# Half of the next stage's norm moved beside an earlier output projection, side work pinned on four engines, statistics a pair later

## The chip, the cores and the metric

The kernel runs on one core of a Trainium2 chip. The metric is the time of one execution on the device in microseconds (us). Five engines of the core matter: PE (TensorE: matmuls, and its weight loads, PEld), DVE (VectorE), ACT (ScalarE), POOL (GpSimd) and SP (SyncE, which here only issues DMAs). Each engine works through its own instructions in a fixed order; engines and DMAs wait for each other through semaphores.

## The reference

One layer of a decoder trunk, then a final norm, on x of 2048 tokens by 1024 channels in float32. Cut to what matters:

```python
h = rmsnorm(x, norm1)
q, k, v, b_gate, c_gate, hc, p = split(h @ w_in)      # 512 128 128 256 256 256 256
attn = sliding_window_attention(q, k, v, sinks, rel_bias)   # window 128, 8 heads
conv = b_gate * causal_depthwise_conv3(c_gate * hc)
pool = per-group map of (trailing mean over 2/4/8/16 - p)
x = x + concat(attn, conv, pool) @ w_out
h2 = rmsnorm(x, norm2)
x = x + square(relu(h2 @ w1)) @ w2                    # 1024 -> 4096 -> 1024
return rmsnorm(x, final_norm)
```

## The kernel before

Everything is held transposed: channels lie on the 128 partitions, tokens along the free axis. Each fp32 product is made of three matmuls on high and low parts (`mm3`: hi·hi, hi·lo, lo·hi), so that one 128x512 tile over 1024 input channels is 24 matmuls of 128x512. High parts are casts on ACT (`wh`, `xh`), low parts are subtractions on POOL for the weights (`wl`, L253) and on DVE for the activations (`xl`, L406).

**Token blocks.** The first stages work on four blocks of 512 tokens, b = 0 to 3. The projection of a block (`proj`, L504; PSUM tiles `pj`) has 14 tiles of 24 matmuls, in the order IN_ORDER; the first ones are k and v, and the loop variable n counts the rest from 0. Beside them run eight attention units, one per n from 0 on: scores on PE (`sc`), scale plus bias on DVE (`s`, L581), maximum on DVE (L588), exponentials on ACT, the reciprocal of the sum and a scaling on DVE (`rd` L593, `s` L594), transposes on PE (`pt`), their high and low parts on ACT and DVE (`pth`, `ptl`, L608), the product with v on PE (`av`), and the heads' output (`ao`, L624). Conv and pool mixers (`do_pmix`: `ppm` on PE, `mxl` on DVE) run on the side. The q tiles' low parts `ql` go through a DMA before the scores can use them.

**Output projection of a block** (`out_proj`, L715; PSUM tiles `po`): eight tiles c = 0 to 7 of 24 matmuls on the mixed heads `mxh`, `mxl`. After each, DVE adds the residual (`xo`, L724), a DMA stores the result to the buffer `x1s` in DRAM, and ACT and POOL sum the squares for the second norm (`acc`, L732). Beside the same eight tiles runs the first norm of block b+1: squares and their sum (c = 0, 1), then `norm_rstd` at c = 2 (a matmul with ones, `pst_n`, and twelve small DVE operations `nt`, `nv`, `ny`, `r` at L316 to L325 that make the inverse root), a transpose on PE (`pr_n`, L333) and a store of the row to DRAM (`row_n`) at c = 3, its load broadcast to 128 partitions (`rb`) at c = 4, and the scaled activations `hf` (L404) with their parts `xh`, `xl` (L405, L406) from c = 5 on, which the projection of block b+1 multiplies.

**The next stage's norm.** The MLP's first stage works in two passes of 1024 tokens with seven products of half-size blocks (names T1 to T4, B11, B21, B22; PSUM tiles `bT`, `bB`), the sums and differences of which are prepared beforehand in DRAM (`x2s_T`, `x2s_B`). For the first pass (blocks 0 and 1) this is `first_blocks(k, step)` for k = 0 to 3. Step 0 loads four 128x512 tiles `xb` from `x1s`; step 1 scales them by the norm's row (four DVE operations, L809, with the broadcast rows `rb2`, loaded once by `first_rows`) and stores three of them; step 2 subtracts four times (`sub`, L763) and stores four results. Over all k that is 16 tile loads, two row loads, 16 scalings, 16 subtractions and 28 stores. In block 3, `first_load` and `first_take` read these back beside its output projection. The tiles `xb` take the place of the norm's input tiles `xr`, which the last block no longer needs.

**What sets the order.** The code is written in one order and a list scheduler with engine estimates places each instruction on its engine; what is in a `tc.issue_after(instruction)` block goes behind that instruction on that instruction's engine, and other engines are not bound by it. DMAs in `late` are put out at the next `w_next` (weights, taken `LEAD` ahead) or `flush`. The table FIRST gives for each k the values of n (in block 3) for its three steps:

```python
FIRST = ((0, 1, 2), (0, 3, 4), (3, 5, 6), (5, 7, 8))
...
            if b + 1 == NB:
                with tc.issue_after(latest[0].ins):
```

`latest[0]` is the last matmul of a projection tile, an instruction of PE.

**After the blocks.** PE runs the MLP's first stage, where events are keyed by (pass, group, step): `on(key, f)`. `norm2_rstd` for the last block (`pst_n`), `norm2_row` and `norm2_bcast` (the second pass's row) are such events. The low part `hlB`, `hlT` of what the first products use is made at L967. The second stage (`o`) ends with the final norm: the residual add, squares on ACT and their sum on POOL (`acc`, L942), the sum over partitions (`pst_n`), a broadcast (`pbc_n`), eight scalings on DVE (L1152) and eight stores on SP (L1156). The last part of this is done for the last 256 tokens alone.

Of the kernel before, what the change touches and what calls it, by code (L numbers as in the profile page):

```python
# [2 lines left out]

# [1 line left out]

# [60 lines left out]
ON_DVE = ((2, 5), (5,))  # L66
SUM_POOL = ("S1", "S2")

FIRST = ((0, 1, 2), (0, 3, 4), (3, 5, 6), (5, 7, 8))

NEARLY = 5

# [7 lines left out]
def f32(ap):  # L80
    return ap.bitcast(F32)
# [3 lines left out]
def tile_trunk(  # L85
# [12 lines left out]
):  # L98
    nc = tc.nc
    pe, act, dve, gp, sp = nc.tensor, nc.scalar, nc.vector, nc.gpsimd, nc.sync  # L100

    cst = ctx.enter_context(tc.tile_pool(name="cst", bufs=1, side="left"))
    wp = ctx.enter_context(tc.tile_pool(name="wp", bufs=2, side="left"))
# [164 lines left out]
    def flush():  # L268

        while late:  # L270
            late.pop(0)()

    def mm3(ps, hi, lo, xh, xl, first, last):
        pe.matmul(ps, hi, xh, start=first, stop=False)  # L274
        pe.matmul(ps, hi, xl, start=False, stop=False)  # L275
        return pe.matmul(ps, lo, xh, start=False, stop=last)  # L276


    prm = cst.tile([P, NPAR], F32, name="prm")
# [26 lines left out]

        return [min(o, w - P) for o in range(0, w, P)]

    def rstd_of(acc, r, offs, psp, tag, name):

        n = r.shape[-1]
        ps = psp.tile([P, T], F32, tag=tag, name=f"pst_{name}")
        for j, o in enumerate(offs):
            pe.matmul(ps[:, j : j + 1], acc[:, o : o + P], ones, start=True, stop=True)
        v, y, t = [cst.tile([P, 6], F32, tag=f"n{a}", name=f"n{a}_{name}", bufs=2)[:, :n] for a in "vyt"]
        dve.tensor_scalar(out=t, in0=ps[:, :n], scalar1=EPS, scalar2=None, op0=ALU.add)  # L316
        dve.tensor_scalar(out=v, in0=ps[:, :n], scalar1=EPS, scalar2=-0.5, op0=ALU.add, op1=ALU.mult)
        dve.tensor_scalar(
            out=y.bitcast(I32), in0=t.bitcast(I32), scalar1=-0.5, scalar2=1597463007.0,
            op0=ALU.mult, op1=ALU.add,  # L320
        )
        for it in range(3):
            dve.tensor_tensor(out=t, in0=y, in1=y, op=ALU.mult)
            dve.tensor_tensor(out=t, in0=t, in1=v, op=ALU.mult)
            dve.scalar_tensor_tensor(  # L325
                out=(r if it == 2 else y), in0=t, scalar=1.5, in1=y, op0=ALU.add, op1=ALU.mult
            )
# [152 lines left out]
    gp.memset(pp[:, :, 0:16], 0.0)  # L480

    first = {}

    latest = [None]

    def start_first(tiles):

        ws = [(w_next(0), w_next(0)) for _ in tiles]
# [10 lines left out]
    def proj(b, i, mid=None, bank=None):  # L499
        if b == 0 and i in first:  # L500
            ps = first[i]
            flush()
        else:
            xh, xl = xhl[b]  # L504
            ps = ps_mm.tile([P, T], F32, tag="mm", name=f"pj{b}_{i}") if bank is None else bank
            for k in range(KC):
                if k % HC == 0:
                    hi, lo = w_next()
                if k == HC and mid:
                    mid()  # L510
                latest[0] = mm3(ps, hi[:, k % HC], lo[:, k % HC], xh[:, k], xl[:, k], k == 0, k == KC - 1)
        return ps

    def scaled(b, i, ps):
# [271 lines left out]

        return plain, sums

    def first_rows():

        rb2[0] = [pB.tile([P, T], F32, tag=t, name=f"rb2_0_{t}") for t in ("rb", "acc")]
        for n in range(2):
            row_load(rb2[0][n], "n2", n * TH)

# [2 lines left out]
    def first_blocks(k, step):  # L797

        if step == 0:
            first_blk[k] = [pA.tile([P, T], F32, tag="xr", name=f"xb{k}_{n}", bufs=KC) for n in range(4)]  # L800
            for n, t in enumerate(first_blk[k]):
                a = n % 2 * TH
                sp.dma_start(t, x1s[k + n // 2 * HC][:, a : a + TH])
            return
        plain, sums = norm2_put(0, k, first_blk[k])
        if step == 1:
            for n, t in enumerate(first_blk[k]):
                m = PG2 + k + n // 2 * HC
                dve.scalar_tensor_tensor(  # L809
                    out=t, in0=t, scalar=prm[:, m : m + 1], in1=rb2[0][n % 2], op0=ALU.mult, op1=ALU.mult  # L810
                )
# [29 lines left out]
    for b in range(NB):  # L841
# [16 lines left out]
        for n, i in enumerate(IN_ORDER[NPRE:]):  # L858
            if n < KC and b + 1 < NB:
                norm_load(b + 1, n)  # L860

            def mid(n=n):
                if 2 <= n < 10:
                    st2[n] = att_trans(*st1.pop(n - 2))

            ps = proj(b, i, mid)
            if b and n == 1:
                norm2_row(b - 1, ps_tr, "tr", tmp(f"row2_{b}"))
            if 2 <= n < 10:
                av = att_av(*st2.pop(n))  # L870
            evac[i](b, scaled(b, i, ps))
            if 2 <= n < 10:
                att_out(*av, dve if n > 5 else gp)
            if n < 8:
                st1[n] = att_scores(b, *units[n])
            if n == 5:
                do_pool(b, 0)
            elif n == 7:
                do_pool(b, 1)
                do_pmix(b, 0)  # L880
            elif n == 9:
# [257 lines left out]
    def final_rstd(p, n, cs):  # L1139
        w = cs.stop - cs.start  # L1140
        offs = starts(w)
        r = cst.tile([P, 6], F32, tag="nr3", name=f"r3_{p}_{n}_{cs.start}", bufs=2)[:, : len(offs)]
        rstd_of(acc3[p, n][:, cs], r, offs, psb, "b", f"n3_{p}_{n}_{cs.start}")
        r3[p, n, cs.start] = r

    def final_bcast(p, n, cs):
        w = cs.stop - cs.start
        rb3[p, n, cs.start] = bcast(r3[p, n, cs.start], w, psb, "b", f"n3_{p}_{n}_{cs.start}")

    def final_mul(p, n, f, cs):  # L1150
# [5 lines left out]
        late.append(lambda: sp.dma_start(outT[f * P : (f + 1) * P, a + cs.start : a + cs.stop], t))  # L1156

    ev = {}
    full = slice(0, TH)
# [155 lines left out]
```

## Time and profile before

| | us |
|---|---|
| three runs of the kernel | 1935.1, 1942.73, 1940.79 (median 1940.79) |
| the profiled execution | 1936.93 |
| its span on the core | 1935.2 |
| busy: PE, DVE, POOL, ACT | 1892.6, 1123.6, 1020.0, 895.9 |
| granted PE clock, mean | 0.99 |

The span is what the trace covers; 1.73 us of the profiled execution lie outside it. In a row of a timeline the columns are: start and duration in us, engine, line, operation, out<-in, partitions x elements and type, count, and in brackets the idle time just before on that engine with what ended it. A row over a stretch of time (of the windows view) has start:end, length, then the busy time and number of instructions of PE, PEld, DVE, ACT and POOL, the granted PE clock, the share of the DMA engines and GB/s. A group's row has its count, and then busy us and mean ns of one.

### The profile page before, as it was taken

The page shows a single profiled execution, that of the slowest core. Times are in us where ns is not written, and L with a number is a line of the kernel's source. Part 1 is how long each engine was busy: PE and PEld are TensorE (multiplying, and loading weights), DVE is VectorE, ACT ScalarE, POOL GpSimd, SP SyncE. Part 2 cuts the span into 40 slices and gives each one's busy share as a digit, 9 for nine tenths or more (in the row PEclk, how much of TensorE's full clock was granted, in tenths as well). Part 3 has the DMA queues.
Part 4 walks back from the last instruction along what each step waited for, and adds up shares of the span by engine and source line. Part 5 has one row for each costly group of instructions (what it writes and reads, how often), then busy time and mean ns, then how long its engine had stood idle before and what let it go on. Part 6 is the DMA issues. An engine that isn't in the chain of part 4 may idle for free.

```text
span 1935.2 us, 25620 instructions
## 1 busy us (share of the span) xinstructions
PE 1892.6 (98%) x8507; PEld 1527.8 (79%) x8507; DVE 1123.6 (58%) x1423; ACT 895.9 (46%) x1640; POOL 1020.0 (53%) x748
## 2 busy tenths in 40 slices
PE   8999999999899999999999999999999999999997
PEld 5877887887687788888888888888888888888887
DVE  5785686585888577756574444442425264533465
ACT  5664674564367344554575545442323222225332
POOL 5666557565463655654464444434565665526521
PEclk9999999999899999999999999999999999999998
DMA  7327316425935779756685655578777566645344
GB/s 255 102 65 225 108 61 217 126 66 174 300 117 178 233 272 335 255 197 212 216 288 194 196 185 189 186 270 279 235 231 240 191 218 200 221 123 169 96 158 134
DMA packets 194136, 373.34 MB, mean 193 GB/s; under 512 B 22167, under 2 KB 30420, under 8 KB 194004
## 3 DMA queue, kind: packets, MB, share of 16 engines
q1 hardware_dynamic: 193768, 371.62, 59.6%
q8 instruction: 67, 1.10, 0.2%
q14 instruction: 65, 0.53, 0.1%
q10 hardware_dynamic: 236, 0.09, 0.0%
HBM read 248.41 MB, written 116.93 MB: 189 GB/s over the span
## 4 chain that ended last, share of the span: by engine, by line
PE 83%; DVE 7%; DMA 6%; issue 2%; ACT 1%; POOL 1%; SPq 1%; DVEq 0%; POOLq 0%; ACTq 0%
PE o L274 11%; PE o L275 11%; PE o L276 11%; PE bT L275 6%; PE bT L276 6%; PE bT L274 6%; PE bB L275 5%; PE bB L274 5%; PE bB L276 5%; PE pj L275 4%; PE pj L276 4%; PE pj L274 4%; DMA x1s<-xo 1%; PE pt L604 1%; DVE xl L406 1%
## 5 line engine op out<-in xcount | busy, mean ns | idle before, releaser
L253 POOL TENSOR_TENSOR wl<-wr,wh 128x512 fp32r<-128x512 f32 x354 | 499.2, 1417 | 502.4 <-ACT wh L252 462.1
L252 ACT CAST wh<-wr 128x512 fp32r<-128x512 f32 x416 | 254.3, 617 | 362.5 <-PE bT L275 66.9
L763 DVE TENSOR_TENSOR bl<-br,bh 128x1024 fp32r<-128x1024 f32 (+2 forms) x144 | 186.8, 1300 | 324.7 <-ACT bh L1111 323.8
L275 PE MATMUL o<-bl,wh 128*128 128x512 f32 (+1 forms) x960 | 363.4, 381 | 0.0
L276 PE MATMUL o<-bh,wl 128*128 128x512 f32 (+1 forms) x960 | 362.7, 381 | 0.0
L274 PE MATMUL o<-bh,wh 128*128 128x512 f32 (+1 forms) x960 | 351.1, 381 | 0.0
L275 PEld LDWEIGHTS o<-bl,wh 128*128 128x128 f32 x960 | 180.9, 188 | 38.3 <-DVE bl L763 0.2
L276 PEld LDWEIGHTS o<-bh,wl 128*128 128x128 f32 x960 | 180.8, 188 | 38.2
L274 PEld LDWEIGHTS o<-bh,wh 128*128 128x128 f32 x960 | 176.3, 188 | 38.0
L276 PE MATMUL bT<-hhT,wl 128*128 128x512 f32 x512 | 203.7, 398 | 0.0
L275 PE MATMUL bT<-hlT,wh 128*128 128x512 f32 x512 | 203.6, 398 | 0.0
L274 PE MATMUL bT<-hhT,wh 128*128 128x512 f32 x512 | 203.4, 398 | 0.0
L274 PE MATMUL pj<-xh,wh 128*128 128x512 f32 x440 | 176.7, 403 | 10.6 <-ACT wh L252 6.7
L275 PE MATMUL pj<-xl,wh 128*128 128x512 f32 x440 | 177.5, 403 | 6.1 <-DVE xl L406 5.8
L276 PE MATMUL pj<-xh,wl 128*128 128x512 f32 x440 | 176.2, 401 | 0.0
L253 POOL TENSOR_TENSOR wl<-s,wh 128x512 fp32r<-128x512 f32 x64 | 91.2, 1426 | 141.5 <-ACT wh L252 130.9
L252 ACT CAST wh<-s 128x512 fp32r<-128x512 f32 x64 | 39.7, 621 | 250.1 <-PE o L275 249.9
L275 PE MATMUL bB<-hlB,wh 128*128 128x512 f32 x384 | 152.3, 397 | 0.7 <-DVE hlB L967 0.7
L274 PE MATMUL bB<-hhB,wh 128*128 128x512 f32 x384 | 152.5, 397 | 0.0
L1111 ACT CAST bh<-br 128x1024 fp32r<-128x1024 f32 (+2 forms) x144 | 123.2, 857 | 63.3 <-PE o L276 57.6
L276 PE MATMUL bB<-hhB,wl 128*128 128x512 f32 x384 | 152.0, 396 | 0.0
L220 POOL TENSOR_TENSOR s<-wr,wr 128x512 f32<-128x512 f32 x64 | 128.5, 2008 | 14.9 <-DMA wr<-in_w_dram 10.2
(188 smaller groups left out, 3388.0 us busy)
## 6 DMA issues: line engine op xcount, KB each, us to landing
wr<-in_w_dram SPq DMA_DIRECT2D x256, 256.0 KB, 3.8
hop_T<-s SPq DMA_DIRECT2D x128, 256.0 KB, 3.1
wr<-in_win_dram SPq DMA_DIRECT2D x112, 256.0 KB, 4.4
hop_B<-h SPq DMA_DIRECT2D x96, 256.0 KB, 3.3
br<-hop_B SPq DMA_DIRECT2D x48, 512.0 KB, 4.4
br<-hop_T SPq DMA_DIRECT2D x48, 512.0 KB, 4.3
wr<-in_wout_dram SPq DMA_DIRECT2D x64, 256.0 KB, 2.9
wr<-ss_T SPq DMA_DIRECT2D x48, 256.0 KB, 2.8
```

Of the source, the lines that this page charges most:

```text
L220: gp.tensor_tensor(out=t, in0=a, in1=b, op=op)
L252: act.copy(hi, src)
L253: eng.tensor_tensor(out=lo, in0=src, in1=f32(hi), op=ALU.subtract)
L274: pe.matmul(ps, hi, xh, start=first, stop=False)
L275: pe.matmul(ps, hi, xl, start=False, stop=False)
L276: return pe.matmul(ps, lo, xh, start=False, stop=last)
L406: dve.tensor_tensor(out=xl[:, k], in0=hf, in1=f32(xh[:, k]), op=ALU.subtract)
L604: pe.transpose(ps[:, m * P : (m + 1) * P], s[:, m, kh * P : (kh + 1) * P], ident)
L763: return dve.tensor_tensor(out=out, in0=a, in1=b, op=ALU.subtract)
L1111: mark["act"] = act.copy(hi, src)
```

## The change

The norm for k = 0 and 1 (`first_rows` and two of the four `first_blocks`) is moved out of block 3's projection and into the output projection of block 2 (b + 2 == NB), where the tiles `pth`, `ptl`, `q0` and `q1` of the attention are not in use. For k = 2 and 3 it stays in block 3, at other values of n, with a second pair of row loads. The order of this work is now tied by `behind()` to the latest instruction on each of ACT, DVE, POOL and SP, and no longer to one of PE. The second norm's statistics at the start of the MLP come one group later. At the kernel's end the last 256 tokens' four squares are no longer added up on POOL: PE sums them in PSUM, with five matmuls for each of two columns in place of one, and the final stores alternate between the queues of SP and ACT.

```diff
-FIRST = ((0, 1, 2), (0, 3, 4), (3, 5, 6), (5, 7, 8))
+FIRST = ((), (), (0, 2, 3), (2, 4, 5))
+BEFORE = ((0, 1, 2), (1, 2, 3))
...
+    sides = {e.engine for e in (act, dve, gp, sp)}
...
+    @contextmanager
+    def behind():
+        with ExitStack() as order:
+            seen = set()
+            for ins in reversed(nc.cur_bb.bb.instructions):
+                if ins.engine in sides and ins.engine not in seen:
+                    seen.add(ins.engine)
+                    order.enter_context(tc.issue_after(ins))
+                    if len(seen) == len(sides):
+                        break
+            yield
...
-    def rstd_of(acc, r, offs, psp, tag, name):
+    def rstd_of(accs, r, offs, psp, tag, name):
...
+        accs = accs if isinstance(accs, list) else [accs]
         for j, o in enumerate(offs):
-            pe.matmul(ps[:, j : j + 1], acc[:, o : o + P], ones, start=True, stop=True)
+            for i, acc in enumerate(accs):
+                pe.matmul(ps[:, j : j + 1], acc[:, o : o + P], ones, start=i == 0, stop=i == len(accs) - 1)
...
-    def first_rows():
-        rb2[0] = [pB.tile([P, T], F32, tag=t, name=f"rb2_0_{t}") for t in ("rb", "acc")]
+    def first_rows(pool, tags, bufs):
+        rb2[0] = [pool.tile([P, T], F32, tag=t, name=f"rb2_0_{t}", bufs=bufs) for t in tags]
...
         if step == 0:
-            first_blk[k] = [pA.tile([P, T], F32, tag="xr", name=f"xb{k}_{n}", bufs=KC) for n in range(4)]
+            if k == 0:
+                first_blk[k] = [pA.tile([P, T], F32, tag=t, name=f"xb{k}_{t}{n}", bufs=3) for t in ("pth", "ptl") for n in range(2)]
+            elif k == 1:
+                qs = [f32(pA.tile([P, 2, T], F32R, tag=f"q{i}", name=f"xb{k}_{i}")) for i in range(2)]
+                first_blk[k] = [q[:, a] for q in qs for a in range(2)]
+            else:
+                first_blk[k] = [pA.tile([P, T], F32, tag="xr", name=f"xb{k}_{n}", bufs=KC) for n in range(4)]
...
-                with tc.issue_after(latest[0].ins):
+                with behind():
                     if n == 0:
-                        first_rows()
+                        first_rows(pB, ("rb", "acc"), 1)
...
         for c in range(KC):
+            if b + 2 == NB:
+                with behind():
+                    if c == 0:
+                        first_rows(pA, ("pth", "ptl"), 3)
+                    for k, at in enumerate(BEFORE):
+                        for step in range(3):
+                            if c == at[step]:
+                                first_blocks(k, step)
...
-    on((0, 0, 2), norm2_rstd, NB - 1, psb, "b")
-    on((0, 1, 4), lambda: norm2_row(NB - 1, psb, "b", um("row2")))
-    on((0, 3, 0), norm2_bcast, 1)
+    on((0, 1, 2), norm2_rstd, NB - 1, psb, "b")
+    on((0, 2, 4), lambda: norm2_row(NB - 1, psb, "b", um("row2")))
+    on((0, 3, 2), norm2_bcast, 1)
...
     cs = slice(TH // 2, TH)
+    w = TH // 2
+    acc3[1, 0] = [acc3[1, 0]]
     for j in range(HC):
-        final_square(1, 0, 2 * j + 1, cs, False)
+        if j % 2 == 0:
+            sq = pG.tile([P, TH], F32, tag="sq", name=f"sql_{j}", bufs=2)
+        t = sq[:, j % 2 * w : j % 2 * w + w]
+        act.activation(t, y_of(1, 2 * j + 1, 0, cs), AF.Square)
+        acc3[1, 0].append(t)
     final_rstd(1, 0, cs)
     final_bcast(1, 0, cs)
     for f in range(KC):
-        final_mul(1, 0, f, cs)
+        final_mul(1, 0, f, cs, act if f % 2 else sp)
         flush()
```

How the instructions now stand, in the order of the engines. Line numbers are those of each kernel; L830 is the old L809, L778 the old L763, L739 the old L724.

DVE in the output projection of block 2, before: after the first two residual adds come the small operations of the first norm of block 3, with nothing of the next stage among them.

```order
L724 TENSOR_TENSOR xo_0_4611<-po_0_4612,xo_0_4611 128x512
L724 TENSOR_TENSOR xo_1_4662<-po_1_4663,xo_1_4662 128x512
L316 TENSOR_SCALAR nt_n_3_4714<-pst_n_3_4707 128x4
L317 TENSOR_SCALAR nv_n_3_4712<-pst_n_3_4707 128x4
L318 TENSOR_SCALAR ny_n_3_4713<-nt_n_3_4714 128x4
L323 TENSOR_TENSOR nt_n_3_4714<-ny_n_3_4713 128x4
L324 TENSOR_TENSOR nt_n_3_4714<-nt_n_3_4714,nv_n_3_4712 128x4
L325 SCALAR_TENSOR_TENSOR ny_n_3_4713<-nt_n_3_4714,ny_n_3_4713 128x4
```

After, the scalings of k = 0 (tiles `xb_pth`, `xb_ptl`) and of k = 1 (`xb_0`, `xb_1`) stand there:

```order
L739 TENSOR_TENSOR xo_0_4623<-po_0_4624,xo_0_4623 128x512
L830 SCALAR_TENSOR_TENSOR xb_pth_4606<-xb_pth_4606,prm,rb_0_pth 128x512
L830 SCALAR_TENSOR_TENSOR xb_pth_4607<-xb_pth_4607,prm,rb_0_ptl 128x512
L830 SCALAR_TENSOR_TENSOR xb_ptl_4608<-xb_ptl_4608,prm,rb_0_pth 128x512
L830 SCALAR_TENSOR_TENSOR xb_ptl_4609<-xb_ptl_4609,prm,rb_0_ptl 128x512
L739 TENSOR_TENSOR xo_1_4684<-po_1_4685,xo_1_4684 128x512
L830 SCALAR_TENSOR_TENSOR xb_0_4669<-xb_0_4669,prm,rb_0_pth 128x512
L830 SCALAR_TENSOR_TENSOR xb_0_4669<-xb_0_4669,prm,rb_0_ptl 128x512
L830 SCALAR_TENSOR_TENSOR xb_1_4670<-xb_1_4670,prm,rb_0_pth 128x512
L334 TENSOR_SCALAR nt_n_3_4747<-pst_n_3_4740 128x4
L335 TENSOR_SCALAR nv_n_3_4745<-pst_n_3_4740 128x4
L830 SCALAR_TENSOR_TENSOR xb_1_4670<-xb_1_4670,prm,rb_0_ptl 128x512
```

Between the residual add of tile 0 and the start of the small operations there are now seven scalings, and one more scaling and four subtractions stand between the small ones; four subtractions more follow the third residual add.

PE in the same projection, before: the transpose `pr_n_3` of the norm's row, which waits for the result `r_3` of the small operations, stands among the matmuls of tile 3 (`po_3`), after 17 of its 24.

```order
L276 MATMUL po_3_4776<-mxh,wl_4665 128x512
L274 MATMUL po_3_4776<-mxh,wh_4664 128x512
L275 MATMUL po_3_4776<-mxl,wh_4664 128x512
L333 MATMUL pr_n_3_4772<-ident,r_3_4706 4x128
L276 MATMUL po_3_4776<-mxh,wl_4665 128x512
L274 MATMUL po_3_4776<-mxh,wh_4664 128x512
```

After, it stands among the matmuls of tile 4, after 14 of its 24:

```order
L292 MATMUL po_4_4871<-mxh,wl_4710 128x512
L290 MATMUL po_4_4871<-mxh,wh_4762 128x512
L291 MATMUL po_4_4871<-mxl,wh_4762 128x512
L351 MATMUL pr_n_3_4816<-ident,r_3_4739 4x128
L292 MATMUL po_4_4871<-mxh,wl_4763 128x512
L290 MATMUL po_4_4871<-mxh,wh_4762 128x512
```

Twenty-one matmuls of 128x512 more stand ahead of it.

On SP, the store of that row (`row_n`) now stands behind the stores of all eight subtractions.

DVE at the start of block 3, before: scalings and subtractions of k = 0 and 1 stand ahead of the evacuation of the keys (`Kd`) and the first `ql`.

```order
L809 SCALAR_TENSOR_TENSOR xb_0_5262<-xb_0_5262,prm,rb_0_rb 128x512
L809 SCALAR_TENSOR_TENSOR xb_2_5264<-xb_2_5264,prm,rb_0_rb 128x512
L809 SCALAR_TENSOR_TENSOR xb_0_5270<-xb_0_5270,prm,rb_0_rb 128x512
L809 SCALAR_TENSOR_TENSOR xb_2_5272<-xb_2_5272,prm,rb_0_rb 128x512
L809 SCALAR_TENSOR_TENSOR xb_3_5273<-xb_3_5273,prm,rb_0_acc 128x512
L763 TENSOR_TENSOR xb_0_5262<-xb_1_5263,xb_0_5262 128x512
```

After, DVE goes there from the last `xl` straight to `Kd` and `ql`; the scalings of k = 2 stand between the softmax of unit 2 and of unit 3:

```order
L608 RECIPROCAL rd_2_0_5475<-den_2_0_5474 128x4
L609 TENSOR_TENSOR s_2_0_5470<-s_2_0_5470,rd_2_0_5475 128x4x256
L830 SCALAR_TENSOR_TENSOR xb_0_5310<-xb_0_5310,prm,rb_0_rb 128x512
L830 SCALAR_TENSOR_TENSOR xb_1_5311<-xb_1_5311,prm,rb_0_acc 128x512
L830 SCALAR_TENSOR_TENSOR xb_2_5312<-xb_2_5312,prm,rb_0_rb 128x512
L830 SCALAR_TENSOR_TENSOR xb_3_5313<-xb_3_5313,prm,rb_0_acc 128x512
L639 TENSOR_TENSOR ao_0_0_5456<-av_0_0_5445,ao_0_0_5456 64x512
L596 SCALAR_TENSOR_TENSOR s_3_0_5581<-sc_3_0_5572,bias 128x4x256
```

Eight scalings and eight subtractions are left to the projection of block 3, all of them behind the first unit's scores.

More of the change, by code (lines that the diff above doesn't have):

```diff
@@ L1 @@
 import math
-from contextlib import ExitStack
+from contextlib import ExitStack, contextmanager
 import numpy as np
@@ L275, in mm3 @@
         pe.matmul(ps, hi, xl, start=False, stop=False)
-        return pe.matmul(ps, lo, xh, start=False, stop=last)
+        pe.matmul(ps, lo, xh, start=False, stop=last)
     prm = cst.tile([P, NPAR], F32, name="prm")
@@ L482, in tile_trunk @@
     first = {}
-    latest = [None]
     def start_first(tiles):
@@ L510, in proj @@
                     mid()
-                latest[0] = mm3(ps, hi[:, k % HC], lo[:, k % HC], xh[:, k], xl[:, k], k == 0, k == KC - 1)
+                mm3(ps, hi[:, k % HC], lo[:, k % HC], xh[:, k], xl[:, k], k == 0, k == KC - 1)
         return ps
@@ L885, in tile_trunk @@
             if b + 1 == NB:
-                with tc.issue_after(latest[0].ins):
+                with behind():
                     if n == 0:
-                        first_rows()
+                        first_rows(pB, ("rb", "acc"), 1)
                     for k, at in enumerate(FIRST):
-                        for step in range(3):
-                            if n == at[step]:
+                        for step, m in enumerate(at):
+                            if n == m:
                                 first_blocks(k, step)
@@ L1142, in final_rstd @@
         r = cst.tile([P, 6], F32, tag="nr3", name=f"r3_{p}_{n}_{cs.start}", bufs=2)[:, : len(offs)]
-        rstd_of(acc3[p, n][:, cs], r, offs, psb, "b", f"n3_{p}_{n}_{cs.start}")
+        a = acc3[p, n]
+        rstd_of([a[0][:, cs]] + a[1:] if isinstance(a, list) else a[:, cs], r, offs, psb, "b", f"n3_{p}_{n}_{cs.start}")
         r3[p, n, cs.start] = r
@@ L1148, in final_bcast, with final_mul @@
         rb3[p, n, cs.start] = bcast(r3[p, n, cs.start], w, psb, "b", f"n3_{p}_{n}_{cs.start}")
-    def final_mul(p, n, f, cs):
+    def final_mul(p, n, f, cs, eng=sp):
         t = y_of(p, f, n, cs)
@@ L1155, in final_mul @@
         a = p * TM + n * TH
-        late.append(lambda: sp.dma_start(outT[f * P : (f + 1) * P, a + cs.start : a + cs.stop], t))
+        late.append(lambda: eng.dma_start(outT[f * P : (f + 1) * P, a + cs.start : a + cs.stop], t))
     ev = {}
```

## The prediction

> **What bounds the kernel now.** I read the page's totals first, then the windows view stage by stage, then the waits of PE, then DVE's timeline where PE waits for it.
>
> ```profile
> span 1935.2 us, 25620 instructions
> PE 1892.6 (98%) x8507; PEld 1527.8 (79%) x8507; DVE 1123.6 (58%) x1423; ACT 895.9 (46%) x1640; POOL 1020.0 (53%) x748
> ```
>
> PE is busy 98% of the span. A change that removes no matmul can win only where PE idles or runs at a reduced clock: 1935.2 − 1892.6 = 42.6 us plus what the clock loses. Where that lies, the windows show (columns: start:end, length, busy of PE, PEld, DVE, ACT, POOL, clock, DMA share, GB/s):
>
> ```profile
> 327.50:430.00 102.50, 101.62 (x504) 83.11 (x502) 68.86 (x95) 63.81 (x150) 66.13 (x60) 1.00 0.40 115
> 430.00:479.10 49.10, 48.79 (x217) 39.05 (x216) 29.42 (x43) 22.16 (x39) 25.07 (x22) 1.00 0.51 155
> 479.10:599.70 120.60, 109.21 (x510) 87.01 (x508) 104.64 (x135) 65.63 (x152) 66.55 (x51) 0.94 0.59 188
> 663.90:1923.40 1259.50, 1255.56 (x5576) 1018.62 (x5575) 649.77 (x777) 523.94 (x839) 628.82 (x416) 1.00 0.65 212
> ```
>
> The rows are block 2's projection, block 2's output projection, block 3's projection and the MLP. The MLP is full. Block 3's projection does the work of block 2's (510 matmuls against 504) and takes 120.6 us instead of 102.5: 18.1 us, the largest loss that the change can reach. There DVE is busy 104.64 of 120.6 us against 68.86 in block 2. Block 2's output projection has 29.42 us of DVE in 49.1, so there is room. The half-clock stretches and PE's waits:
>
> ```profile
> 486.40:493.20 6.80, 3.89 (x9) 2.65 (x9) 6.80 (x7) 1.96 (x4) 3.85 (x3) 0.50 0.86 262
> 595.60:602.40 6.80, 6.35 (x19) 4.95 (x20) 5.87 (x10) 4.40 (x8) 1.28 (x1) 0.50 0.04 15
> 660.50:663.90 3.40, 3.40 (x9) 2.62 (x9) 1.21 (x2) 1.79 (x4) 0.00 (x0) 0.50 0.94 305
> ```
> ```profile
> PE pj L275 <- DVE xl L406: 5.8, 7, 2.9
> PE sc L577 <- DMA q<-ql: 3.6, 5, 2.2
> PE pst_n L314 <- POOL acc L942: 3.5, 1, 3.5
> ...
> PE pst_n L314 <- POOL acc L732: 1.2, 1, 1.2
> ```
>
> The `xl` and `ql` waits belong to block 3's first 40 us, where DVE is late; the clock halves after them (486.4) and again when the attention runs out without cover (595.6).
>
> **A. Block 3's projection.** DVE's timeline, first and last softmax operation of block 2, then of block 3, with what follows to the end:
>
> ```profile
> 355.40 1.23 DVE L581 SCALAR_TENSOR_TENSOR s<-sc,bias 128x1024 f32<-128x1024 f32 x1 [5.22 <-PE sc L578]
> 421.75 1.23 DVE L594 TENSOR_TENSOR s<-s,rd 128x1024 f32<-128x1024 f32 x1
> ```
> ```profile
> 528.35 1.23 DVE L581 SCALAR_TENSOR_TENSOR s<-sc,bias 128x1024 f32<-128x1024 f32 x1
> 591.51 1.23 DVE L594 TENSOR_TENSOR s<-s,rd 128x1024 f32<-128x1024 f32 x1
> 592.65 0.74 DVE L708 SCALAR_TENSOR_TENSOR mxl<-ppm,prm,mxh 128x512 fp32r<-128x512 f32 x1
> 593.32 1.86 DVE L688 SCALAR_TENSOR_TENSOR po<-ps,prm,pp 64x512 f32<-64x512 f32 x2
> 595.21 0.69 DVE L624 TENSOR_TENSOR ao<-av,ao 64x512 f32<-64x512 f32 x1
> ```
> ```profile
> L763 DVE TENSOR_TENSOR xb<-xb,xb 128x512 f32<-128x512 f32 x16 | 13.1, 839 | 0.1
> L809 DVE SCALAR_TENSOR_TENSOR xb<-xb,prm,rb_rb 128x512 f32<-128x512 f32 x8 | 8.4, 1075 | 1.6 <-DMA xb<-x1s 1.6
> L809 DVE SCALAR_TENSOR_TENSOR xb<-xb,prm,rb_acc 128x512 f32<-128x512 f32 x8 | 8.1, 1013 | 7.9 <-DMA xb<-x1s 7.9
> ```
> ```profile
> 355.40:423.00 67.60, 50.59 (x63) 1.00 0.24 78
> 528.35:592.74 64.39, 55.10 (x69) 1.00 0.38 124
> ```
> ```profile
> DVE rd L593 <- ACT s L590: 14.0, 8, 3.1
> ```
>
> The first scale stands 355.40 − 327.5 = 27.9 us after the start in block 2, 528.35 − 479.1 = 49.25 in block 3: the `xb` operations stand ahead of `Kd` and `ql` there. In the changed order they don't, so I take 27.9 for the start. From first scale to last scaling it takes 67.6 us in block 2. Into this chain now come all operations of k = 2 and 3: eight scalings at (8.4 + 8.1)/16 = 1.03 and eight subtractions at 13.1/16 = 0.82, 8.2 + 6.6 = 14.8 us. The windows are those of DVE alone in the two chains: 50.59 of 67.6 us busy in block 2, 17 idle, and 55.10 of 64.39 in block 3, 9.3 idle. In block 2's chain 14.0 of the 17 are waits of the reciprocal for the exponentials on ACT (the last row, of DVE's waits in 355 to 424); such waits remain in block 3, and I let its 9.3 stand. From below, then: 50.6 + 14.8 + 9.3 = 74.7. From above, nothing hides: 67.6 + 14.8 = 82.4. In the new order the scalings stand behind a unit's scaling and not between its maximum and its reciprocal, where DVE idles; only some subtractions come into such holes. I take the middle, 78.5. Behind the last scaling lay 599.7 − 592.7 = 7.0 us; the new order puts `mxl` (0.74) and `po` (1.86) ahead, leaving 4.4 us: transposes, `ptl`, `ao`. So the stage ends after 27.9 + 78.5 + 4.4 = 110.8 us: **a gain of 9.8** (bounds 120.6 − 107.0 = 13.6 and 120.6 − 114.7 = 5.9; block 2's 102.5 is the floor). DVE remains the late engine: 104.64 − 14.8 = 90 us busy.
>
> **B. Block 2's output projection.** What the moved work delays:
>
> ```profile
> 446.91 0.69 DVE L724 TENSOR_TENSOR xo<-po,xo 128x512 f32<-128x512 f32 x1 [2.01 <-PE po L276]
> ...
> 450.02 1.22 DVE L324 TENSOR_TENSOR nt_n<-nt_n,nv_n 128x4 f32<-128x4 f32 x1
> ...
> 453.52 0.16 DVE L325 SCALAR_TENSOR_TENSOR r<-nt_n,ny_n 128x4 f32<-128x4 f32 x1
> ```
> ```profile
> 454.85 0.27 PE L333 MATMUL pr_n<-ident,r 128*4 128x128 f32 x1
> 449.93 1.30 POOL L253 TENSOR_TENSOR wl<-wr,wh 128x512 fp32r<-128x512 f32 x1
> 466.40 1.41 DVE L404 SCALAR_TENSOR_TENSOR hf<-xr,prm,rb 128x512 f32<-128x512 f32 x2 [3.14 <-DMA rb<-row_n]
> L763 DVE TENSOR_TENSOR xb<-xb,xb x16: 670/679/1769, 499.1 to 540.6; 128x512 f32<-128x512 f32 x16
> L809 DVE SCALAR_TENSOR_TENSOR xb<-xb,prm,rb_acc x8: 737/752/1776, 474.9 to 529.5; 128x512 f32<-128x512 f32 x8
> ```
>
> Eight scalings and four subtractions now precede `r`: 8 × 1.03 + 4 × 0.82 = 11.5 us, at their minima (0.737 and 0.670 us) 8.6. DVE idled 2.01 us there, so `r`, which ended at 453.7, comes 6.6 to 9.5 us later. `pr_n` came 1.2 us behind `r` and stands 21 matmuls later on PE; at 49.10/217 = 0.226 us each that is 4.7. PE then waits between 6.6 − 5.9 = 0.7 and 9.5 − 5.9 = 3.6 us, with all matmuls of the tile queued behind, and a half-clock stretch of 3.4 us as at 660.5, worth 1.7, may follow. I take **a loss of 2.3** (0 to 5.3, the latter with the clock). Further on, `row_n` is stored behind the subtractions' stores. The last four subtractions follow `r` and an `xo`, 0.7 + 4 × 0.8 = 4 us, so that `rb` lands about 7 us later and `hf` starts near 473. Two `hf`, an `xo` and an `xl` at 0.7 each then give the first `xl` at 476, some 3 us before block 3's first tile at 479.1 asks for it; and without `xb` among them DVE does not trail there any more. The four subtractions behind `xo` 2 delay nothing PE asks for. Loads and stores: 24 DMAs of 256 KB, 6.3 MB, add 128 GB/s to the 155 of the 49.1 us, 283 together; 305 GB/s stand in the row of 660.5, so they fit. Their cover is that weights are loaded ahead.
>
> Rows 449.93 on POOL and 450.02 on DVE, 1.30 and 1.22 us at the same time, the latter for 128x4 values that take 0.16 elsewhere, show that a DVE operation may last as long as a neighbour on POOL. The Trainium skill, page SBUF — State Buffer, section Who interferes with whom, says that a DVE operation with two SBUF inputs contends with a GpSimd operation that reads SBUF; the trace agrees. The means, 1.03 and 0.82 against minima of 0.737 and 0.670, already hold the usual share of such meetings, so I keep them; every one of the twelve meeting a POOL operation is a rival below.
>
> **C. Start of the MLP.** PE's 1.2 us wait at `pst_n` and the 3.4 us at half clock (660.5) may go: at most 1.2 + 1.7 = 2.9 us.
>
> ```profile
> 661.89 0.62 ACT L966 CAST hhT<-xu_T 128x512 fp32r<-128x512 f32 x1 [6.07 <-DMA xu_T<-x2s_T]
> 669.74 1.17 DVE L967 TENSOR_TENSOR hlB<-xu_B,hhB 128x512 fp32r<-128x512 f32 x1
> ```
>
> The first products still want `hhT`, loaded until 661.9, and `hlB` until 670.9, which don't depend on the statistics. PE would reach them earlier and wait there: **0** (−1 to +2.9).
>
> **D. The tail.**
>
> ```profile
> 1919.52 1.42 DVE L942 TENSOR_TENSOR y<-o,y 128x256 f32<-128x256 f32 x4 [2.70 <-PE o L276]
> 1923.71 1.02 PE L314 MATMUL pst_n<-ones,acc 128*128 128x1 f32 x4 [3.52 <-POOL acc L942]
> 1922.09 0.42 ACT L1136 ACTIVATE sq<-y 128x256 f32<-128x256 f32 x1 [0.38 <-POOL acc L942]
> 1928.78 3.77 SPq L1156 DMA_DIRECT2D out_dram<-y  x8
> ```
>
> Four POOL additions vanish, and the squares no longer wait for them: the last `y` ends at 1920.94, its square (0.42) at about 1921.5. Of ten matmuls with ones, one of column 0 and five of column 1 follow that: six pieces of two entries, 12 × 1.02/4 = 3.1 us, or less if the clock is up. `pst_n` ended at 1924.7, so 0.1 to 1.8 us; I take 1.0. The eight stores end 3.77 us after 1928.78; two queues issue them in half the time, but the last scaling sets the last issue: 0.6. **Gain 1.6** (0.7 to 2.4).
>
> **Sum.** 9.8 − 2.3 + 0 + 1.6 = 9.1 us against the profiled 1936.93: 1927.8. The median of the runs, 1940.79, lies 3.9 above that execution: 1931.7 by it. I forecast 1930.
>
> **Rivals.**
> - *Full gain.* Block 3 gets block 2's pace, 102.5 us, when the k = 2 and 3 work falls into DVE's 17 us of idle time: 18.1 − 2.3 + 1.6 = 17.4 us, 1919.5 to 1923.4. For it: 17 idle us against 14.8 of work. Against it: 14 of the 17 lie between maximum and reciprocal, where the order puts little.
> - *Given back.* Each of the twelve operations ahead of `r` meets one of POOL and lasts 1.3 us: 15.6 in place of 11.5, PE waits 15.6 − 2.0 − 5.9 = 7.7, the clock takes 1.7 more, and 9.8 − 9.4 + 1.6 = 2.0 us are left: 1934.9 to 1938.8, no change. For it: the pair of 1.30 and 1.22 us at 450. Against it: POOL is busy 25.07 of 49.1 us there, so half the operations find it idle. This is what the section of the Trainium skill named above would give if every issue collided.
> - *Slower.* SP's queue: the plain and the difference stores wait on DVE, and the weight loads, the row's store and its broadcast load behind them wait too. Once `hf` starts later than about 476 (466.4 plus 7 plus the 3 to spare), each us more stops PE at block 3's first tile; it needs 476 + 9.1 + 9.7 ≈ 495, a queue held 19 us, to end over 0.5% slower: 1951 or more. For it: DVE holds these stores back by 11.5 us in the worst place. Against it: weights are loaded ahead, and 24 more issues at 3.77/8 = 0.47 us are 11.3 us in all.
> - *It doesn't do what it says*: that would need `xb` at block 3's start again; the order shows them behind the first softmax.
>
> **Numbers.** Forecast (A near the middle) 0.5, full gain 0.19, given back 0.2, slower 0.11. About 0.5% (9.7 us, 1931.1) is what a measurement of this kernel can tell from no change; the forecast's own case lies on that line and splits 0.3 to 0.2. The chances: faster 0.3 + 0.19 = 0.49; same 0.2 + 0.2 = 0.4; slower 0.11. The range takes in the full gain and the given-back case: 1918 to 1941. The likeliest case alone: 1924 to 1936.
>
> **What would show it.** A: block 3's projection 107 to 115 us, the first softmax some 28 us after its start, no `xl` wait of PE over 1 us, DVE near 90 us busy. B: one wait of PE at `pr_n` in tile 4 of 0.7 to 3.6 us, `hf` at about 473. C: the wait for `pst_n` gone, one for `hlT` or `hlB` grown. D: `pst_n` at 1922 plus shift, and the span's end 1 to 2 us nearer to the last matmul. The prediction is wrong if block 3 starts with waits for `xl` longer than the 5.8 us of before, or if the chain of softmaxes takes over 82 us.

## The result and the profile after

| | us |
|---|---|
| before, 17 runs | 1938.02 (1935.1 to 1942.73) |
| changed, 17 runs | 1945.35 (1941.55 to 1948.71) |
| ratio | 1.0037, 95% interval 1.003 to 1.0044 |
| profiled execution of the changed kernel, span | 1943.51, 1941.7 |

The change made the kernel about 7 us slower, where 1930 was forecast. The page's totals, the stages (block 2's projection, its output projection, block 3's projection, its output projection) and three stretches at half clock after the change (a fourth, of 3.4 us, begins at 602.2):

```profile
span 1941.7 us, 25645 instructions
PE 1895.5 (98%) x8523; PEld 1530.8 (79%) x8523; DVE 1136.6 (59%) x1423; ACT 896.2 (46%) x1640; POOL 1021.3 (53%) x744
```
```profile
327.30:432.80 105.50, 102.14 (x504) 83.16 (x502) 70.88 (x97) 63.82 (x150) 68.21 (x61) 1.00 0.41 117
432.80:486.20 53.40, 50.52 (x217) 40.18 (x216) 43.82 (x57) 23.02 (x40) 31.16 (x23) 0.97 0.78 248
486.20:603.90 117.70, 105.58 (x504) 85.63 (x503) 96.69 (x120) 63.69 (x149) 66.57 (x50) 0.96 0.49 149
603.90:653.40 49.50, 49.03 (x207) 38.58 (x206) 36.58 (x46) 28.42 (x50) 23.46 (x16) 0.98 0.72 239
```
```profile
465.70:469.10 3.40, 3.40 (x10) 2.64 (x9) 3.30 (x5) 1.29 (x3) 2.31 (x2) 0.50 0.89 245
585.20:592.00 6.80, 4.11 (x10) 3.25 (x11) 6.74 (x8) 1.53 (x3) 3.36 (x3) 0.50 0.44 146
670.50:677.30 6.80, 6.08 (x12) 3.46 (x12) 6.45 (x7) 5.00 (x10) 6.00 (x4) 0.50 0.80 311
```

DVE is 13.0 us busier (1136.6 against 1123.6) with the same 1423 instructions: the same work takes longer where it now stands, and 8.2 of the 13.0 us are in the 32 `xb` operations (30.1 us before, 38.3 after). Block 3's projection gained 2.9 us; block 2's output projection lost 4.3. PE's waits, after the change and, in the last row, before it:

```profile
PE pj L290 <- DVE bo L668: 5.7, 1, 5.7
PE pj L291 <- DVE xl L424: 5.7, 5, 1.8
...
PE pr_n L351 <- DVE r L343: 2.6, 1, 2.6
```
```profile
PE pj L274 <- DVE bo L653: 0.8, 1, 0.8
```

The wait at `pr_n` is the one forecast. The wait for `bo` (the conv mixer's gate, which frees a PSUM bank that the next projection tile needs) was 0.8 us before and is 5.7 now. A table of the stage lengths, each from PE's first matmul of a stage to its first of the next, in this trace and in those of the runs below (one trace of each kernel; the two columns of the changed kernel differ by up to 1.3 us):

| us | before | changed | changed, again | all in block 3 | half left out | in the waits |
|---|---|---|---|---|---|---|
| block 2, projection | 102.4 | 105.4 | 104.1 | 102.0 | 103.6 | 102.7 |
| block 2, output projection | 49.1 | 53.4 | 53.4 | 49.1 | 49.2 | 53.1 |
| block 3, projection | 120.6 | 117.7 | 118.0 | 109.8 | 117.6 | 108.2 |
| block 3, output projection | 48.6 | 49.4 | 49.4 | 58.5 | 49.4 | 49.5 |
| MLP, first stage | 635.0 | 638.3 | 639.2 | 633.8 | 637.3 | 634.1 |
| MLP, second stage and final norm | 651.9 | 650.1 | 650.4 | 650.3 | 650.6 | 651.2 |

### The profile page after: what moved, and what is told of

Read it like the earlier page. It is cut to its first block, busy times and chain, and to the rows that moved or that the text cites. A ratio compares the mean times of both kernels' runs of the same rounds, so it can differ in the third digit from the quotient of the medians.

```text
span 1941.7 us, 25645 instructions
## 1 busy us (share of the span) xinstructions
PE 1895.5 (98%) x8523; PEld 1530.8 (79%) x8523; DVE 1136.6 (59%) x1423; ACT 896.2 (46%) x1640; POOL 1021.3 (53%) x744
## 4 chain that ended last, share of the span: by engine, by line
PE 77%; DVE 6%; DMA 5%; issue 2%; ACT 1%; SPq 1%; POOL 0%; DVEq 0%; ACTq 0%; POOLq 0%
PE o L290 11%; PE o L291 11%; PE o L292 11%; PE bT L292 6%; PE bT L291 6%; PE bT L290 6%; PE bB L291 4%; PE bB L290 4%; PE bB L292 4%; PE pj L291 3%; PE pj L290 3%; PE pj L292 3%; DMA x1s<-xo 1%; DMA xu_T<-x2s_T 1%; DVE xl L424 1%
## 5 line engine op out<-in xcount | busy, mean ns | idle before, releaser
L256 POOL TENSOR_TENSOR wl<-wr,wh 128x512 fp32r<-128x512 f32 x354 | 504.5, 1431 | 503.1 <-ACT wh L255 465.3
L778 DVE TENSOR_TENSOR bl<-br,bh 128x1024 fp32r<-128x1024 f32 (+2 forms) x144 | 186.7, 1299 | 325.3 <-ACT bh L1140 324.5
L290 PEld LDWEIGHTS o<-bh,wh 128*128 128x128 f32 x960 | 176.5, 189 | 38.3 <-ACT bh L1140 0.4
```

The source lines that it names most:

```text
L256: eng.tensor_tensor(out=lo, in0=src, in1=f32(hi), op=ALU.subtract)
L778: return dve.tensor_tensor(out=out, in0=a, in1=b, op=ALU.subtract)
```

## The experiments

Each kernel ran beside the kernel before on the same chip; the ratios are to that one. Theory 1: the loss sits where the moved and the remaining half delay DVE's results that PE waits for. Theory 2: transfers land later in many places.

**One number: the last subtractions later.**
```diff
-FIRST = ((), (), (0, 2, 3), (2, 4, 5))
+FIRST = ((), (), (0, 2, 3), (2, 4, 8))
```


> The changed kernel with one number changed: the four subtractions of k = 3 stand at n = 8 instead of n = 5 in block 3. Theory 1 (the loss sits in block 3's chain on DVE and in block 2's output projection): the gate's evacuation bo no longer stands behind two subtractions of 3.42 us, so PE's wait of 5.7 us for it and most of the 6.8 us at half clock go, worth 3.4; the subtractions come back behind the last softmax and cost 2 to 3. Block 3's projection 111 to 113 us instead of 117.7, the run 5 to 7 us under the changed kernel, about 1939. Theory 2 (diffuse: transfers land later by 1.5 us here and there in the changed kernel, block 2's start and the MLP's start 3 us each): no more than 2 us, about 1944.

Measured 1940.34 us, ratio 1.0012 (1.0003 to 1.0021). The time fell as theory 1 has it, but not where: block 3's projection took 115.7 us, PE still waited 3.7 us for `bo`, and its output projection grew to 53.2, to 168.9 together against 167.2. By the trace the largest gain lies in the MLP's first stage, 633.4 us. `bo` now came behind a scaling of 2.22 us. So the two subtractions were part of the wait for `bo`, and taking them away there alone brings nothing to block 3: DVE is late there anyway.

**The statistics back in their old place.**
```diff
-    on((0, 1, 2), norm2_rstd, NB - 1, psb, "b")
+    on((0, 0, 2), norm2_rstd, NB - 1, psb, "b")
...  (row and broadcast likewise)
```


> The changed kernel with the three events of the second norm's statistics at the MLP's start put back to where they were. Theory 1: the 3.3 us that the MLP's first 25 us lost in the one trace come from a weight load that landed 1.4 us later ahead of POOL's sum S, on which DVE's residual add and all that is behind it wait; the statistics have no part in it, and the time is that of the changed kernel, 1945 +- 1.5. Rival: the later statistics cost the 3.3 us; then 1942.

Measured 1941.6 us, 1.0016 (1.0007 to 1.0025): the rival's number. But this kernel's trace has 637.7 us in the MLP's first stage against 638.3, so the trace does not show the gain where the rival puts it.

**The new tail alone, on the kernel before.**
```diff
-        final_square(1, 0, 2 * j + 1, cs, False)
+        act.activation(t, y_of(1, 2 * j + 1, 0, cs), AF.Square)
+        acc3[1, 0].append(t)
...
-        final_mul(1, 0, f, cs)
+        final_mul(1, 0, f, cs, act if f % 2 else sp)
```

> The kernel before with the new tail alone (four squares summed by PE, final stores on two queues). Both theories: 1.8 us less than before, the difference of the two traces from the second stage's first matmul to the end (651.9 and 650.1 us): 1936.2, ratio 0.999. If the gain in the trace was chance: ratio 1.000.

Measured 1935.61 us, 0.9987 (0.9978 to 0.9996). The tail gains 2.4 us by the runs (0.8 to 4.3), 0.8 by this kernel's trace, 1.8 by the changed one's.

**All four k in block 3, with the new order.**
```diff
-FIRST = ((), (), (0, 2, 3), (2, 4, 5))
-BEFORE = ((0, 1, 2), (1, 2, 3))
+FIRST = ((0, 1, 2), (0, 3, 4), (3, 5, 6), (5, 7, 8))
...  (the BEFORE loop and its tiles go)
```


> The changed kernel without the moved half: all four k stand in block 3 at the old values of n, but tied by the new order to ACT, DVE, POOL and SP; tail and statistics as changed. Theory 1: block 2's output projection is back at 49.1 us (4.3 less), but all 32 operations stand in the softmax chain of block 3 at 1.2 to 1.36 us each: the chain is 86.4 + 16 x 1.28 = 107 us, the projection some 135 us, and the time about 1945 - 4 + 17 = 1958. Rival (the order on the four engines is harmless or good, and the moved half alone did the harm): about 1936, the kernel before less the tail's 1.8.

Measured 1935.56 us, 0.9988 (0.9978 to 0.9998): the rival holds, and theory 1's price for the chain fell. With twice as much side work in it, block 3's projection took 109.8 us and both of its stages 168.3, only 1.2 more than in the changed kernel. Its chain, from first scale to last scaling, took 81.9 us with 22 of the 32 operations in it, which took 1.04 us each in the mean; in the changed kernel it took 86.4 with 16 of them at 1.28. So the moved half brought block 3 next to nothing, and the order on four engines did no harm. Run again,

> The kernel with all four k in block 3 and the new order (1935.6 before), looked at once more for its stages: the same stage lengths within 1.5 us, 109.8 and 58.5 us for block 3's two stages.

it gave 110.0 and 58.5 us, and 1935.91.

**The moved half behind the first norm's small operations.**
```diff
-BEFORE = ((0, 1, 2), (1, 2, 3))
+BEFORE = ((0, 3, 4), (1, 3, 4))
```


> The changed kernel with the moved half's scalings at c = 3 and its subtractions at c = 4 of block 2's output projection, so that all of them stand behind the small operations of the first norm. Theory 1 (the half was put ahead of r, and PE waits for r at pr_n): the wait of 2.8 us and the 3.4 us at half clock behind it go, the output projection is back from 53.4 to 49.1 us, and the time is 4.4 us under the changed kernel's 1945.3, about 1941. Rival (DVE has no room anywhere in that stage): hf and xl come later by as much, PE's wait for xl at block 3's start grows from 2 to 5 or 6 us, and the time is 1944 to 1946.

Measured 1943.62 us, 1.0031 (1.002 to 1.0043): the rival. The wait at `pr_n` went, and `hf` still came late, since DVE reached it only at 478:

```profile
477.44 0.69 DVE L778 TENSOR_TENSOR xb<-xb 128x512 f32<-128x512 f32 x1
478.05 3.49 DVE L422 SCALAR_TENSOR_TENSOR hf<-xr,prm,rb 128x512 f32<-128x512 f32 x2
```

PE then waited at block 3's first tiles; output projection and projection took 51.9 and 120.6 us.

**The moved half left out.**
```diff
+            if b == 1 and n < 7:
+                for k in range(2):
+                    sp.dma_start(x2s[0, OPS[n]][:, k], x1s[n][:, 0:T])
...
-            if b + 2 == NB:
-                with behind():
...  (all of the BEFORE loop)
```


> The changed kernel with the moved half left out: no loads, scalings, subtractions and stores of k = 0 and 1 in block 2's output projection (their part of the MLP's input is filled by plain copies in block 1, so the output is not the reference's). What it saves is the whole price of the moved half. Theory 1: PE's wait at pr_n (2.8 us) and the half clock behind it (1.7) go and the output projection is back at 49.1; hf comes at 466 again instead of 480, and the wait for xl at block 3's start goes (2 us); block 3's chain stays at 86 us: 6 to 7 us less than the changed kernel, 1938 to 1939. Rival (the half costs only its wait at pr_n, and block 3 takes up whatever time it gets): 1941 or more.

Measured 1941.62 us, 1.0025 (1.0016 to 1.0034). The total is no measure of the half: the 14 copies stretched block 1's projection to 108.6 us from 102.6. By stages, the output projection is back at 49.2, as theory 1 has it, and block 3 is unchanged (117.6 and 49.4), where theory 1 expected 2 us. So the half costs 4.3 us in its own stage, and its absence gives block 3 nothing.

**The remaining half in DVE's waits.** The 16 operations go, one to three at a time, between an attention unit's maximum and its reciprocal. The loads of k = 3 now leave together with those of k = 2.
```diff
-FIRST = ((), (), (0, 2, 3), (2, 4, 5))
+FIRST = ((), (), (0,), (0,))
+HOLES = (0, 1, 3, 3, 3, 2, 3, 1)
...
         last = dve.tensor_reduce(out=nm, ...)
         (four exponentials on ACT)
+        for _ in range(n_fill):
+            with tc.issue_after(last.ins):
+                last = fill.pop(0)()
+        with tc.issue_after(last.ins):
             dve.reciprocal(out=rd, in_=den)
```


> The changed kernel with the 16 operations of k = 2 and 3 in block 3 put one to three at a time between the maximum and the reciprocal of an attention unit, where DVE waits for the exponentials on ACT (14 us of such waits in block 2). Theory 1 (they lengthen the softmax chain because they stand outside these waits): the chain from first scale to last scaling falls from 86.4 us to 70 to 75, the wait for bo goes, block 3's projection with its output projection takes 155 to 159 us instead of 167.2, and the time is 8 to 12 us lower, 1933 to 1937. Rival (the two stages together take 167 to 169 us in every kernel so far, so something other than the chain sets them): 1943 or more.

Measured 1927.49 us, 0.9944 (0.9932 to 0.9957): 16 to 18 us under the changed kernel and 11 under the one before, more than expected. DVE's waits and windows in the two chains, changed kernel first (columns of a window: length, DVE busy, clock, DMA share, GB/s), and the chain's first and last rows:

```profile
DVE rd L608 <- ACT s L605: 9.0, 6, 3.1
514.30:600.70 86.40, 74.23 (x84) 0.96 0.43 140
514.32 1.23 DVE L596 SCALAR_TENSOR_TENSOR s<-sc,bias 128x1024 f32<-128x1024 f32 x1 [4.77 <-PE sc L593]
599.49 1.21 DVE L609 TENSOR_TENSOR s<-s,rd 128x1024 f32<-128x1024 f32 x1
```
```profile
DVE rd L616 <- ACT s L609: 2.0, 3, 1.1
513.00:585.40 72.40, 67.75 (x81) 1.00 0.45 153
513.02 1.23 DVE L600 SCALAR_TENSOR_TENSOR s<-sc,bias 128x1024 f32<-128x1024 f32 x1 [5.02 <-PE sc L597]
584.15 1.22 DVE L617 TENSOR_TENSOR s<-s,rd 128x1024 f32<-128x1024 f32 x1
```

The reciprocal's wait for the exponentials is 2.0 us instead of 9.0, the chain 72.4 instead of 86.4, and block 3's two stages take 157.7 us instead of 167.2. Of the 14 us that the chain lost, 7.5 are idle time of DVE and 6.5 are busy time: the 16 operations took 18.3 us instead of 20.5, and some others no longer stand between the two ends. The earlier loads are not what did it: in the changed kernel DVE idled 0.1 us in all ahead of these 16 operations. The MLP's first stage is 634.1 with the statistics still late. Run again,

> The kernel with k = 2 and 3 in DVE's waits (1927.5 before), looked at once more: the chain from first scale to last scaling 72 +- 1 us, block 3's two stages 157.7 +- 1, time 1927 +- 2.

it gave 156.7 us for the two stages and 1928.46.

**The waits with other edits.** To the kernel with the 16 operations in the waits:
```diff
-BEFORE = ((0, 1, 2), (1, 2, 3))
+BEFORE = ((0, 3, 4), (1, 3, 4))
...
-    on((0, 1, 2), norm2_rstd, NB - 1, psb, "b")
+    on((0, 0, 2), norm2_rstd, NB - 1, psb, "b")
```

> Three edits to the changed kernel together: the moved half behind r (as in late_before), k = 2 and 3 in DVE's waits for the exponentials (as in holes), the statistics at the MLP's start back in their old place (3.9 us by the run of that edit alone). Theory 1: the three add, 1945.3 - 4.4 - 10 - 3.9 = 1927 (1923 to 1931), below both kernels. Rival (the two stages of block 3 are held by something else): 1937.

Measured 1928.72 us, 0.9947 (0.9934 to 0.9961): no better than the waits alone, so the three do not add; the late half again brought nothing.

With the second of these alone:

> The kernel with k = 2 and 3 in DVE's waits, and the statistics at the MLP's start back in their old place. In the changed kernel that edit brought 3.9 us by the runs. If the later statistics cost by themselves: 1923.5. If they cost only where block 3's end leaves the loads of the first products late (MLP's first stage 638 us in the changed kernel, 634 in the kernel with k = 2 and 3 in DVE's waits): no gain here, 1927 to 1929, since PE waits 1.4 us for the squares' sum again.

Measured 1925.35 us, 0.9941 (0.9928 to 0.9955). This is the lowest time of the study; from 0.9944 it can't be told apart, so the statistics' place brought nothing that these runs can show here (the two intervals leave room for some 4 us either way).

**The changed kernel once more.**

> The changed kernel once more, for a second trace. Theory 1: the output projection of block 2 (53.4 us), PE's 5.9 us before the gate's evacuation bo, block 3's projection (117.7) and the tail (650.1) come back within 0.5 us, since they follow from the order; block 2's projection (105.4) and the MLP's first stage (638.3) may differ by 1 to 4 us, if they hang on when a transfer lands. Time 1945 +- 1.5.

Measured 1943.75 us, 1.0028 (1.0018 to 1.0038). The stages of order came back (53.4, 118.0, 650.4; the wait for `bo` 5.7 in both), and so, within 1.3 us, did the two that I had put down to when a transfer lands: 104.1 and 639.2. Against this second measurement the late subtractions (1.0012) and the old place of the statistics (1.0016) are 3 and 2 us faster, not 5 and 4, and their intervals overlap with its own, so neither gain is clear.

## Why the prediction was wrong, by its steps

**A, first and last step: right.** The first scale stands 28.1 us after block 3's start; 27.9 was taken. Behind the last scaling lie 3.2 us; 4.4 was taken.

**A, second step: failed.** This is the largest miss. The chain took 86.4 us instead of 78.5, over the bound of 82.4 and over the 82 that the prediction had named as its sign of being wrong. The term that it had too small is the price of the 16 operations: sum and bound took the mean duration of `xb` operations from the place that they left. After the change, in the chain:

```profile
L778 DVE TENSOR_TENSOR xb<-xb,xb 128x512 f32<-128x512 f32 x8 | 9.6, 1206 | 0.1
L830 DVE SCALAR_TENSOR_TENSOR xb<-xb,prm,rb_rb 128x512 f32<-128x512 f32 x4 | 6.1, 1522 | 0.0
L830 DVE SCALAR_TENSOR_TENSOR xb<-xb,prm,rb_acc 128x512 f32<-128x512 f32 x4 | 4.8, 1196 | 0.0
```

That is 20.5 us where 14.8 stood in the sum, 5.7 of the 7.9 us that were missed; with it the bound would have been 67.6 + 20.5 = 88.1. DVE idled 12.2 us in the chain, where the lower sum let 9.3 stand. What sets one operation's length shows beside POOL's rows: first two operations that started while POOL was at work, then one with POOL starting 0.2 us behind it:

```profile
563.11 3.35 POOL L256 TENSOR_TENSOR wl<-wr,wh 128x512 fp32r<-128x512 f32 x2 [0.71 <-ACT wh L255]
563.53 1.77 DVE L830 SCALAR_TENSOR_TENSOR xb<-xb,prm,rb_rb 128x512 f32<-128x512 f32 x1
565.23 1.78 DVE L830 SCALAR_TENSOR_TENSOR xb<-xb,prm,rb_acc 128x512 f32<-128x512 f32 x1
```
```profile
552.87 0.67 DVE L778 TENSOR_TENSOR xb<-xb,xb 128x512 f32<-128x512 f32 x1
553.08 1.63 POOL L644 TENSOR_TENSOR mxl<-ao,mxh 64x512 fp32r<-64x512 f32 x1 [1.88 <-ACT mxh L643]
```

Over the whole trace, 21 of the 32 `xb` operations start while a POOL operation runs and take 1.45 us in the mean, up to 1.8; the other eleven take 0.67 to 0.74. Before it was 10 of 32, and none of the other 22 took over 0.76. Each of these 31 ends 0.55 to 0.62 us after the POOL operation that it had met, however much of that was left. The Trainium skill, page SBUF — State Buffer, section Who interferes with whom, says that a DVE operation with two SBUF inputs contends with a GpSimd operation that reads SBUF; the traces agree. No run took POOL's work away, but the lengths follow POOL's ends too closely for chance. Three of the 16, all of them subtractions, stood between a maximum and its reciprocal (at 557.57, and two at 583.82); that only some would, the prediction had said, and the run with all 16 in the waits shows what this place was worth.

**Left out of A: what waits for DVE.** The prediction named transposes, `ptl` and `ao` as what waits for DVE, and not the evacuations that free PSUM for PE. Two subtractions stood ahead of `bo`:

```profile
581.14 1.21 DVE L603 TENSOR_REDUCE nm<-s 128x4 f32<-128x1028 f32 x1
582.27 1.62 DVE L256 TENSOR_TENSOR wl<-wr,wh 128x512 fp32r<-128x512 f32 x1
583.82 3.42 DVE L778 TENSOR_TENSOR xb<-xb,xb 128x512 f32<-128x512 f32 x2
587.16 0.68 DVE L668 TENSOR_TENSOR bo<-pj,cy 128x512 f32<-128x512 f32 x1
```

PE stood for 5.7 us, from 582.2 on. The clock halved at 585.2, during this wait, for 6.8 us; PE was busy for 4.1 of them, so some 2.1 were lost. In the order of instructions this could have been read: `bo` came behind the subtractions. It is no loss on top of the chain's: with these subtractions behind the last softmax, the two stages of block 3 took 168.9 us.

**B: the size within its range, its path longer than said.** PE waited 2.6 us at `pr_n`, and 3.4 us at half clock followed (465.7), all of them busy, 1.7 lost: 4.3, within 0 to 5.3, where 2.3 was taken.

```profile
465.12 0.16 DVE L343 SCALAR_TENSOR_TENSOR r<-nt_n,ny_n 128x4 f32<-128x4 f32 x1
465.34 0.27 PE L351 MATMUL pr_n<-ident,r 128*4 128x128 f32 x1 [2.58 <-DVE r L343]
471.15 0.29 SPq L358 DMA_DIRECT2D row_n<-row  x1
478.06 0.69 DVE L739 TENSOR_TENSOR xo<-po,xo 128x512 f32<-128x512 f32 x1 [6.76 <-DMA xo<-in_xT_dram]
480.41 2.87 DVE L422 SCALAR_TENSOR_TENSOR hf<-xr,prm,rb 128x512 f32<-128x512 f32 x2 [1.65 <-DMA rb<-row_n]
```

Counted from the stage's start (430.0 before, 432.8 now), `r` came 8.8 us later, within 6.6 to 9.5, and the row's store left SP 8.8 us later (459.56 before), behind the stores of the subtractions. But `hf` started 11.2 us later and not 7: from the row's store to `hf` it took 9.3 us instead of 6.8. The 3 us to spare were used up, and PE waited 1.8 us for `xl` in block 3, where the prediction wanted no such wait over 1 us (before it was 3.8; the 5.8 us in the prediction are those of all blocks). The path of the rival "slower" was open, at a smaller size than it asked for.

**C: failed.** 0 was taken, 3.3 us were lost (4.3 in the second trace). Before, the last store ahead of the residual load `xo` that waits for it, this load, the weight load that POOL's sum `S` waits for, `S`, and the first `xu` loads; then the same after:

```profile
642.85 0.32 SPq L725 DMA_DIRECT2D x1s<-xo  x1
645.69 0.33 SPq L722 DMA_DIRECT2D xo<-in_xT_dram  x1
646.12 0.38 SPq L197 DMA_DIRECT2D wr<-in_w_dram  x1
650.96 1.29 POOL L210 TENSOR_TENSOR S<-wr,wr 128x512 f32<-128x512 f32 x1 [3.78 <-DMA wr<-in_w_dram]
656.56 1.89 SPq L965 DMA_DIRECT2D xu_T<-x2s_T  x4
```
```profile
648.87 0.38 SPq L740 DMA_DIRECT2D x1s<-xo  x1
652.75 0.33 SPq L737 DMA_DIRECT2D xo<-in_xT_dram  x1
653.17 0.39 SPq L200 DMA_DIRECT2D wr<-in_w_dram  x1
657.55 1.29 POOL L213 TENSOR_TENSOR S<-wr,wr 128x512 f32<-128x512 f32 x1 [5.52 <-DMA wr<-in_w_dram]
663.18 1.91 SPq L994 DMA_DIRECT2D xu_T<-x2s_T  x4
```

Counted from the stage's start (648.3 and 653.4), the store left SP 4.5 us ahead of it instead of 5.5, since another residual load now stands in front of it, and the load behind it left 3.9 us after the store instead of 2.8. So the weight load left 0.2 us ahead of the stage's start instead of 2.2, `S` began 1.6 us later in the stage, and the `xu` loads, which stand behind the stores of `S` in SP's queue, left after 9.8 us instead of 8.2. The wait at `pst_n` went and small waits for `hhT`, `hlT` and `hlB` came in its place, as C had said: PE idled 2.0 us in the first 30 us, as before. But the clock stood at half for 6.8 us instead of 3.4, 1.7 more lost; 37 us into the stage the changed kernel was 2.3 us behind. Another 1.0 us (1.9 in the second trace) went some 340 us into the stage, at a wait for `hlT` that the kernel before and the one with the new tail alone don't have. What each of these comes from is open: in the kernels whose block 3 ends otherwise the stage took 633.4 to 636.5 us, but where only the moved half came later, behind the first norm's small operations, it took 636.1, and no run separates the causes. Theory 2 is neither shown nor excluded for these losses. Open too is the 1.7 to 3 us that block 2's projection lost in both traces to a wait for `xl`: ahead of block 2's output projection every engine has its instructions in the same order as before. So it is in all kernels but the one with the half left out, and their traces spread from 102.0 to 105.4 us for this stage.

**D: right.** 1.8 us between the traces, 2.4 by the runs of the tail alone; 1.6 was taken.

In sum: 9.8 were counted in block 3's projection and 2.9 came; 0 in the MLP's first stage and −3.3 came; −2.3 in block 2's output projection and −4.3 came; nothing in block 2's projection and in block 3's output projection, and −3.0 and −0.8 came in the first trace; 1.6 at the tail and 1.8 came. Of the 16.4 us between the forecast's sum, a gain of 9.1, and the runs' loss of 7.3, the chain of block 3 is the largest part.

## What to carry to other kernels

Side work on an in-order engine was priced here by what stands behind it, and not by its amount: a kernel with all 32 operations in block 3 was 8 to 10 us faster than the one that moved 16 of them out, and 16 put into the waits for another engine took 9.5 us off two stages. Look for the waits inside the critical chain and order the work into them; pinned behind the latest instruction, 13 of 16 came outside the waits. When a wait ends at a transfer, look which load it was: here not the last one issued, but the one before it. Take an operation's duration from the place where it will stand, with the neighbours that it will have there, and list for every moved operation the evacuations that come after it.

## What the hardware showed that I had not expected

A DVE operation of 128x512 float32 on two SBUF tiles took 0.67 to 0.76 us when no POOL operation was running at its start. One that started while a POOL operation ran ended 0.55 to 0.62 us after that operation's end and took up to 1.8 us; this held for all 31 such `xb` operations of the two traces, and the 32 took 38.3 us in sum instead of 30.1. One that had started 0.2 us ahead of POOL's kept its own length (0.67 us at 552.87, 0.74 at 562.87). In the kernel with the operations in the waits, one met two POOL operations in a row and took 3.1 us.

A wait of PE of 2.6 us (until 465.3) was followed by 3.4 us at half clock (from 465.7). In the wait of 5.7 us the clock halved while PE still waited (at 585.2, the wait ending at 587.9), and it stayed at half for 6.8 us.
